# Moving stores to other queues and reordering the loads of an attention layer's input stage

## The chip, the cores and the metric

The program runs on one core of a Trainium2 chip. The core has a matrix engine (PE), a vector engine (DVE), a scalar engine (ACT), a general engine (POOL) and an engine that mostly issues DMAs (SP). Each engine takes its instructions strictly in the order in which they were written down for it; an instruction that waits holds everything behind it on that engine. A DMA is issued from the queue of SP, ACT or POOL; the issuing instruction stands in that engine's order like any other, and waits there for its source. The metric is the device time of one execution, in microseconds (us), lower being better.

## The reference, cut to what matters

Two layers on a latent stream `x` (1024 tokens x 1024 channels) and a context stream `ctx` (256 tokens). Layer 0 is multi-head latent attention, layer 1 a Hyena long convolution. What is computed around the change:

```python
shift, scale, gate = split(silu(c) @ ada_w[i] + ada_b[i], 3)      # adaLN, for each layer i
a  = modulate(rmsnorm(x,   norm_g[0]), shift,   scale)            # h * (1 + scale) + shift
ac = modulate(rmsnorm(ctx, norm_g[0]), shift_c, scale_c)
cq, ckv, k_rope, gate = split(a @ w_in, ...)                      # layer 0's input projections
h  = sin-MLP(features) @ w_out * exp(-t * deltas)                 # Hyena's filters, from the weights alone
spec = rfft(k_circ)                                               # their spectra, used only in layer 1
```

The filter spectra don't depend on `x`; the kernel computes them in layer 0's input stage, beside the projections.

## The kernel before, in words

`layer0_in` is the input stage; after it come attention, its output projection, and the Hyena layer. Everything is float32, products are made from a high and a low part with three matmuls each (`mm3`, lines L119 to L121). Activations lie with channels on partitions, in tiles of 128x512, the two halves of the tokens apart.

Three streams of work are interleaved in `layer0_in`:

- **The normalised input.** `load_x` loads a half of `x` (8 tiles), `rms` squares it on ACT (L380), sums over partitions on PE and forms the reciprocal root; `spread` puts that into a PSUM bank R (L414), and `modulate` makes the high and low part of the modulated input from it (DVE L421, ACT L422, DVE L423; 8 times for each half and, in narrower tiles, for the context).
- **adaLN.** `ada` loads blocks of `ada_w` (L156) and multiplies them with silu(c) in four packed column groups (L128). Layer 0's shift and scale (32 loads of 256 KB into `pg` tiles) come first, since `modulate` needs their result `gs`; layer 1's shift and scale and both gates come later, through two buffers `aw` of 512 KB each.
- **The filters.** `filters` loops over 8 groups g of channels. For each it makes 8 blocks j (matmuls `ph` L318/L319; a load `dec` through two buffers, L314; DVE `kk` L321, `kp`, `km`), and then the ring: DVE builds eight blocks `blk` (L222, L225), each is split by ACT into `bh` (L96) and by DVE into `bl` (L97), multiplied by the tables `fm` (`u`), brought from PSUM by ACT into one of two buffers `ko` (L340), and stored to DRAM as `kd` by two DMAs (L351; for one of the eight also two of `kx`, L353). The tables `fm` are loaded once, from POOL's queue (L295).

The projections take their weights through `weights()`: a load `wr` (L112), an ACT cast and a DVE subtraction. `gates` stores its result to `gate_d` (L600), `hilo_out` stores the compressed keys to `ckv_d` and `kr_d` (L514, L515). Except for `fm`, all loads and stores of this stage are issued from SP's queue. A scheduler sets the order of the instructions on each engine when the program is built, starting from the order in which the generators are advanced: one step of `filt` at a time, and one step of `todo` for every two of those. `keep_in_program_order` and `issue_after` pin an instruction; in the kernel before, `late` pinning is used only in the final norm.

Of the kernel before, what the change touches and what calls it, by code (L numbers as in the profile page):

```python
# [11 lines left out]
F32 = mybir.dt.float32  # L12
F32R = mybir.dt.float32r
AF = mybir.ActivationFunctionType
ALU = mybir.AluOpType
# [4 lines left out]
P = 128  # L20
D = 1024
L = 1024
LC = 256
NK = L + LC
KD = D // P
# [30 lines left out]
class Net:  # L56
# [85 lines left out]
        self.adac = [(self.cst.tile([P, 24, 2], F32, name=f"adac{i}"), self.cst.tile([P, KD, 2], F32, name=f"gs{i}"))  # L142
                     for i in range(2)]

    def ada(self, parts, page, bank, width):

        nc = self.nc
        ps = bank()
        for k in range(KD):
            cols = []  # L150
            for layer, first, n in parts:
                for s in range(0, n * 512, width):
                    wd = min(width, n * 512 - s)
                    w = page(wd)
                    o = 512 * first + s
                    nc.sync.dma_start(out=w, in_=self.a["adaw"][layer, k, :, o : o + wd])  # L156
                    cols += [w[:, j : j + 512] for j in range(0, wd, 512)]
            self.packed([(ps[32 * q : 32 * q + 32, :], self.sc[:, k, :], w, k == 0, k == KD - 1)
                         for q, w in enumerate(cols)])
            yield  # L160
        row = page(512)
        nc.scalar.copy(out=row, in_=ps)
        tp = bank().rearrange("p (j c) -> p j c", j=4)
        for j in range(4):
            nc.tensor.transpose(out=tp[:, j], in_=row[:, j * P : (j + 1) * P], identity=self.ident)
        q = 0
        for layer, first, n in parts:
            res, gs = self.adac[layer]
            for r in range(2):
                c = slice(4 * first, 4 * first + 4 * n)  # L170
                nc.vector.tensor_tensor(out=res[:, c, r].rearrange("p (q j) -> p j q", j=4),
                                        in0=tp[:, :, 32 * q + r : 32 * (q + n) : 32],
                                        in1=self.col(f"b{layer}", 4 * first, 4 * n).rearrange("p (q j) -> p j q", j=4),
                                        op=ALU.add)
                if first == 0:
                    nc.vector.scalar_tensor_tensor(out=gs[:, :, r], in0=res[:, 8:16, r], scalar=1.0,
                                                   in1=self.col(f"g{layer}", 0, 8), op0=ALU.add, op1=ALU.mult)
            q += n
# [105 lines left out]
    def filters(self, psum, pt_h, pt_u, side):  # L284
# [7 lines left out]
        for c in (slice(13, 19), slice(19, 25), slice(0, 7), slice(7, 13)):  # L292
            for i in range(2):
                nc.gpsimd.tensor_copy(out=fm[i][0:1, c.start, 0:1], in_=last[0:1, 0:1])
                nc.gpsimd.dma_start(out=fm[i][:, c], in_=a["fm"][i][:, c])  # L295
# [12 lines left out]
        for g in range(KD):  # L308
            wh, wl = nxt
            kp = [gp.tile([P, 4, CS], F32, tag="rg", name=f"kp{i}") for i in range(2)]  # L310
            km = [gp.tile([P, 4, CS], F32, tag="rg", name=f"km{i}") for i in range(2)]
            for j in range(8):
                dec = rp.tile([P, 2, 1, P], F32, tag="dec", name="dec", bufs=2)
                nc.sync.dma_start(out=dec, in_=a["dec"][g, j])  # L314
                ps = psum.tile([P, 2, 2, P], F32, tag=pt_h, name="ph")
# [21 lines left out]
            def emit(i, b):  # L337
# [10 lines left out]
                    nc.vector.memset(ko[0:1, 1], 0.0)  # L348
                for o in range(2):
                    oc = slice(P * o, P * o + P)  # L350
                    nc.sync.dma_start(out=self.kd[o, g // 2, :, r0 : r0 + 2, cl], in_=ko[:, :, oc])  # L351
                    if i == 0:
                        nc.sync.dma_start(out=self.kd[o, g // 2, :, 2, cl], in_=kx[:, oc])  # L353
# [64 lines left out]
    def modulate(self, x, R, gs, sh, hi, lo):  # L418
# [3 lines left out]
        nc.scalar.activation(out=hi, in_=x, func=AF.Identity, bias=sh)  # L422
        nc.vector.scalar_tensor_tensor(out=lo, in0=x, scalar=sh, in1=hi, op0=ALU.add, op1=ALU.subtract)  # L423

    def project(self, srcs, bank):

        nk = len(srcs[0][0])
# [27 lines left out]
    def layer0_in(self):  # L455
# [28 lines left out]
            for k in range(4):  # L484
                nc.sync.dma_start(out=xc[k], in_=a["ctxT"][:, 2 * k : 2 * k + 2, :])

        load_x(0)
        rx = [self.rms(x[0], 512, bank, page)]
        filt.send(x[0][7])
        for n, _ in enumerate(self.ada([(0, 0, 4)], lambda n: page(), abank, 512)):  # L490
            next(filt)
            if n == 7:
                load_x(1)
                rx.append(self.rms(x[1], 512, bank, page))
        load_c()
        xcs = [xc[k // 2][:, LC * (k % 2) : LC * (k % 2) + LC] for k in range(KD)]
        rc = self.rms(xcs, LC, bank, page)
        ax = []
        for xs, r in zip(x, rx):
            R = self.spread(r, 4, bank)  # L500
            hl = [[], []]
            for k in range(KD):
                hi, lo = page(F32R), page(F32R)
                self.modulate(xs[k], R, gs[:, k, 0:1], res[:, k, 0:1], hi, lo)
                hl[0].append(hi)
                hl[1].append(lo)
            ax.append(hl)

        def hilo_out(t, n, dsts):

            w = t.shape[-1]
            hi, lo = page(F32R)[:, :w], t.bitcast(F32R)
            self.split(t[:n], hi[:n], lo[:n])
            nc.sync.dma_start(out=dsts[0], in_=hi.bitcast(F32)[:n])  # L514
            nc.sync.dma_start(out=dsts[1], in_=lo.bitcast(F32)[:n])  # L515

        def normed(xs, g, dst, sl, sbuf=False):
            n = sl.stop - sl.start
# [10 lines left out]

        def context():  # L530

            R = self.spread(rc, 2, bank)
            ac = [[], []]
            for k in range(0, KD, 2):
                hi, lo = page(F32R), page(F32R)
                for q in range(2):
                    sl = slice(LC * q, LC * q + LC)
                    self.modulate(xcs[k + q], R[:, :LC], gs[:, k + q, 1:2], res[:, k + q, 1:2], hi[:, sl], lo[:, sl])
                    ac[0].append(hi[:, sl])
                    ac[1].append(lo[:, sl])  # L540
            yield
# [52 lines left out]
        def gates(ms):  # L594
            for m in ms:
                bs = yield from self.project(ax, bank)
                for b, sl in zip(bs, halves):
                    t = st()
                    act.activation(out=t, in_=b, func=AF.Silu)
                    nc.sync.dma_start(out=self.gate_d[m, :, sl], in_=t)  # L600
                yield

        def work():
            gen = chain(self.ada([(1, 0, 4)], awt, abank, 1024), self.ada([(0, 4, 2), (1, 4, 2)], awt, abank, 1024))
            for _ in gates(range(0, 3)):
                next(gen, None)
                yield
            yield from latent_kv()
            for _ in gates(range(3, 5)):
                next(gen, None)  # L610
                yield
            yield from context()
            for _ in gates(range(5, 6)):
                next(gen, None)
                yield
            for _ in gen:
                pass

        todo = work()
        n = 0  # L620
        for step, _ in enumerate(filt):
            while n * 120 < (step + 1) * 60:
                next(todo, None)
                n += 1
        for _ in todo:
            pass
        raws = []
        for c in (slice(1152, 2176), slice(0, 768), slice(768, 1152)):
# [819 lines left out]
```

## Time and profile before

| | us |
|---|---|
| median of three runs (lowest, highest) | 1737.97 (1730.38, 1744.37) |
| the profiled execution | 1731.71 |
| its span on the core | 1729.9 |
| PE busy, of the span | 1633.5 |
| DVE busy | 1442.2 |
| ACT busy | 766.3 |
| POOL busy | 16.0 |

The span is the time from the first to the last instruction on the core; 1.8 us of the execution lie outside it. Busy times of an engine are unions of its instructions. The input stage reaches from 0 to 430.4 us, where the first matmul of the attention stage (`pj` from `ckv` and `wc`) starts. The rows "SPq" are issues of DMAs on SP's queue; a row with "xN" merges N instructions in a row.

### The profile page before, as it was taken

To read this page: it belongs to the slowest core of one execution; us is meant where nothing else is said; L and a number is where in the kernel's file an instruction comes from. 1 tells how busy PE (TensorE), PEld (TensorE's weight loads), DVE (VectorE), ACT (ScalarE), POOL (GpSimd) and SP (SyncE) were. 2 spreads that over 40 slices of the span, in tenths; PEclk is the share of its full clock that TensorE was granted. 3 is DMA by queue.
4 is the path that set the end of the run, shared out by engine and by line. 5 is a ranking of instruction groups with operands and counts; after the bars stand their busy time and mean duration, and the time that the engine had idled before them with its cause. 6 is when DMAs were issued, how large, how long until landed. Compare 5 with 4: busy or idle time off the path is not lost.

```text
span 1729.9 us, 22940 instructions
## 1 busy us (share of the span) xinstructions
PE 1633.5 (94%) x8160; PEld 1299.5 (75%) x8160; DVE 1442.2 (83%) x2558; ACT 766.3 (44%) x1337; POOL 16.0 (1%) x43
## 2 busy tenths in 40 slices
PE   5899897899999999999999999999999999999996
PEld 2467676787788788788787777888888888887874
DVE  4886979895699899899899456999999999999856
ACT  4533444445455465555555345433433433343313
POOL 1000000000000000000000010000000000000000
PEclk9899999899999999999999999999999999999998
DMA  9777664436101001010014771332332332244545
GB/s 342 256 231 222 200 187 120 138 89 206 28 27 37 25 32 38 19 33 25 25 56 132 232 254 64 101 98 83 101 115 83 104 106 89 95 122 134 180 142 197
DMA packets 140759, 206.15 MB, mean 119 GB/s; under 512 B 13578, under 2 KB 71649, under 8 KB 140516
## 3 DMA queue, kind: packets, MB, share of 16 engines
q1 hardware_dynamic: 137508, 194.00, 35.7%
q0 software_dynamic: 3136, 10.69, 1.9%
q8 instruction: 64, 1.05, 0.3%
q14 instruction: 51, 0.42, 0.1%
HBM read 148.92 MB, written 53.61 MB: 117 GB/s over the span
## 4 chain that ended last, share of the span: by engine, by line
PE 75%; DVE 10%; DMA 9%; ACT 3%; issue 2%; SPq 1%; DVEq 0%; ACTq 0%
PE pj L121 12%; PE pj L119 12%; PE pj L120 12%; DMA dec<-in_dec 2%; PE O L120 2%; PE S L119 2%; PE O L119 2%; PE S L826 2%; PE O L121 2%; PE apx L762 2%; PE S L825 2%; PE S L121 2%; PE S L120 2%; PE apx L763 2%; PE fu L119 2%; PE fy L119 2%
## 5 line engine op out<-in xcount | busy, mean ns | idle before, releaser
L96 ACT CAST w<-wr 128x512 fp32r<-128x512 f32 (+1 forms) x149 | 90.7, 609 | 259.5 <-PE pj L120 129.5
L119 PE MATMUL pj<-a,w 128*128 128x512 f32 x512 | 203.1, 397 | 1.7 <-ACT a L422 1.6
L121 PE MATMUL pj<-a,w 128*128 128x512 f32 x512 | 203.1, 398 | 0.0
L120 PE MATMUL pj<-a,w 128*128 128x512 f32 x512 | 203.0, 397 | 0.0
L828 ACT ACTIVATE p<-S 128x512 f32<-128x512 f32 x160 | 95.7, 598 | 148.2 <-DVE acc L835 69.5
L97 DVE TENSOR_TENSOR w<-wr,w 128x512 fp32r<-128x512 f32 (+1 forms) x149 | 98.8, 671 | 54.7 <-ACT w L96 54.6
L96 ACT CAST bh<-raw 128x512 fp32r<-128x512 f32 x128 | 77.1, 620 | 89.1 <-DVE raw L1071 71.0
L119 PEld LDWEIGHTS pj<-a,w 128*128 128x128 f32 x512 | 96.4, 188 | 22.0 <-ACT a L422 2.4
L120 PEld LDWEIGHTS pj<-a,w 128*128 128x128 f32 x512 | 96.5, 188 | 19.9 <-DVE a L423 0.2
L121 PEld LDWEIGHTS pj<-a,w 128*128 128x128 f32 x512 | 96.6, 189 | 19.5 <-issue 0.8
L97 DVE TENSOR_TENSOR p<-p 128x512 fp32r<-128x512 f32 x160 | 109.4, 684 | 1.5 <-ACT p L96 1.2
L764 DVE TENSOR_REDUCE cm<-apx 128x1 f32<-128x512 f32 (+1 forms) x192 | 107.1, 591 | 3.8 <-PE apx L763 3.1
L835 DVE TENSOR_TENSOR acc<-acc,p 128x512 f32<-128x512 f32 x144 | 98.7, 685 | 7.6 <-ACT p L828 6.7
L121 PE MATMUL pj<-pg,w 128*128 128x512 f32 (+1 forms) x248 | 96.5, 389 | 8.7 <-DVE w L97 8.6
L96 ACT CAST p<-p 128x512 fp32r<-128x512 f32 x160 | 99.5, 622 | 4.8
L119 PE MATMUL pj<-pg,w 128*128 128x512 f32 (+1 forms) x248 | 95.7, 389 | 2.7 <-ACT pg L422 2.7
L120 PE MATMUL pj<-pg,w 128*128 128x512 f32 (+1 forms) x248 | 96.6, 389 | 0.6 <-DVE pg L423 0.6
L97 DVE TENSOR_TENSOR bl<-raw,bh 128x512 fp32r<-128x512 f32 x128 | 84.7, 686 | 9.1 <-ACT bh L96 9.0
L119 PE MATMUL u<-bh,fm 128*128 128x256 f32 (+1 forms) x200 | 68.2, 342 | 12.2 <-ACT bh L96 9.5
L762 PE MATMUL apx<-kn,qn 128*128 128x512 f32 (+1 forms) x192 | 69.0, 364 | 2.2 <-DVE cm L764 1.9
L321 DVE TENSOR_TENSOR kk<-ph,dec 128x512 f32<-128x512 f32 x64 | 42.6, 684 | 33.2 <-DMA dec<-in_dec 26.6
L763 PE MATMUL apx<-krh,r 128*128 128x512 f32 (+1 forms) x192 | 67.1, 357 | 0.0
(312 smaller groups left out, 4408.9 us busy)
## 6 DMA issues: line engine op xcount, KB each, us to landing
aw<-in_adaw SPq DMA_DIRECT2D x32, 512.0 KB
kd<-ko SPq DMA_DIRECT2D x128, 128.0 KB
wr<-in_hw SPq DMA_DIRECT2D x64, 256.0 KB
kt<-kd SPq DMA_DIRECT2D x56, 256.0 KB
wr<-in_w SPq DMA_DIRECT2D x34, 256.0 KB
dec<-in_dec SPq DMA_DIRECT2D x64, 128.0 KB
pg<-in_adaw SPq DMA_DIRECT2D x32, 256.0 KB
wr<-in_wo SPq DMA_DIRECT2D x32, 256.0 KB
```

The costliest lines, as they stand in the source:

```text
L96: self.nc.scalar.copy(out=hi, in_=raw)
L97: self.nc.vector.tensor_tensor(out=lo, in0=raw, in1=hi, op=ALU.subtract)
L119: mm(out, lhsT=w[0], rhs=x[0], start=start, stop=False)
L120: mm(out, lhsT=w[0], rhs=x[1], start=False, stop=False)
L121: self.last = mm(out, lhsT=w[1], rhs=x[0], start=False, stop=stop)
L321: nc.vector.tensor_tensor(out=kk, in0=ps, in1=dec.broadcast_to([P, 2, 2, P]), op=ALU.mult)
L762: mm(b[:, :w], lhsT=qn[0][:, c], rhs=kn[0][:, o : o + w], start=True, stop=False)
L763: mm(b[:, :w], lhsT=r1[:, c], rhs=krh[:, o : o + w], start=False, stop=True)
L764: v.tensor_reduce(out=cm[:, t, i : i + 1], in_=b[:, :w], axis=AX.X, op=ALU.max)
L825: mm(S, lhsT=krh[:, c], rhs=r1, start=False, stop=False)
L828: act.activation(out=p, in_=S, func=AF.Exp, scale=ASCALE)
L835: v.tensor_tensor(out=acc, in0=acc, in1=p, op=ALU.add)
```

## The change

Six edits, all in the input stage:

1. The stores `kd` and `gate_d` are issued from ACT's queue, `ckv_d` and `kr_d` from POOL's.
2. Layer 0's adaLN loads: four of the eight k (16 of 32 loads) are written ahead of the load of x's second half, the others behind it. Only three instead of eight filter steps are taken beside them.
3. The tables `fm` are loaded inside the first group, at j = 4. They wait for `last`, a tile of x, which DVE has by then overwritten.
4. x is multiplied by its reciprocal root as soon as that is known (`normalize`, one DVE product per tile), and `shifted` replaces `modulate`: ACT forms the high part from x * gs + shift directly, DVE forms the same in place (a tensor_scalar) and subtracts. The context's `rms` moves into `context()`.
5. The later adaLN work no longer advances inside `work()` but every second step from the eighth on; its loads keep their program order, and its packed matmuls are pinned behind the last projection or filter matmul.
6. The generator `ada` yields between the loads and the matmuls.

```diff
-    def ada(self, parts, page, bank, width):
+    def ada(self, parts, page, bank, width, late=True):
...
-                    nc.sync.dma_start(out=w, in_=self.a["adaw"][layer, k, :, o : o + wd])
+                    dma = nc.sync.dma_start(out=w, in_=self.a["adaw"][layer, k, :, o : o + wd])
+                    if late:
+                        self.tc.keep_in_program_order(dma)
                     cols += [w[:, j : j + 512] for j in range(0, wd, 512)]
-            self.packed([(ps[32 * q : 32 * q + 32, :], self.sc[:, k, :], w, k == 0, k == KD - 1)
-                         for q, w in enumerate(cols)])
             yield
+            with self.behind() if late else ExitStack():
+                self.packed([(ps[32 * q : 32 * q + 32, :], self.sc[:, k, :], w, k == 0, k == KD - 1)
+                             for q, w in enumerate(cols)])
...
             for j in range(8):
+                if (g, j) == (0, 4):
+                    for c in (slice(13, 19), slice(19, 25), slice(0, 7), slice(7, 13)):
+                        for i in range(2):
+                            nc.gpsimd.tensor_copy(out=fm[i][0:1, c.start, 0:1], in_=last[0:1, 0:1])
+                            nc.gpsimd.dma_start(out=fm[i][:, c], in_=a["fm"][i][:, c])
...
-                    nc.sync.dma_start(out=self.kd[o, g // 2, :, r0 : r0 + 2, cl], in_=ko[:, :, oc])
+                    nc.scalar.dma_start(out=self.kd[o, g // 2, :, r0 : r0 + 2, cl], in_=ko[:, :, oc])
...
+    def normalize(self, xs, r, bank):
+
+        n = xs[0].shape[-1]
+        R = self.spread(r, n // P, bank)
+        for x in xs:
+            self.nc.vector.tensor_tensor(out=x, in0=x, in1=R[:, :n], op=ALU.mult)
+
+    def shifted(self, x, gs, sh, hi, lo):
+
+        nc = self.nc
+        nc.scalar.activation(out=hi, in_=x, func=AF.Identity, scale=gs, bias=sh)
+        nc.vector.tensor_scalar(out=x, in0=x, scalar1=gs, scalar2=sh, op0=ALU.mult, op1=ALU.add)
+        nc.vector.tensor_tensor(out=lo, in0=x, in1=hi, op=ALU.subtract)
...
-        load_x(0)
-        rx = [self.rms(x[0], 512, bank, page)]
+        for h, xs in enumerate(x):
+            load_x(h)
+            self.normalize(xs, self.rms(xs, 512, bank, page), bank)
+            if h == 0:
+                first = self.ada([(0, 0, 4)], lambda n: page(), abank, 512, False)
+                for _ in range(4):
+                    next(first)
         filt.send(x[0][7])
-        for n, _ in enumerate(self.ada([(0, 0, 4)], lambda n: page(), abank, 512)):
-            next(filt)
-            if n == 7:
-                load_x(1)
-                rx.append(self.rms(x[1], 512, bank, page))
+        for n, _ in enumerate(first):
+            if n < 3:
+                next(filt)
...
-            nc.sync.dma_start(out=dsts[0], in_=hi.bitcast(F32)[:n])
+            nc.gpsimd.dma_start(out=dsts[0], in_=hi.bitcast(F32)[:n])
...
-                    nc.sync.dma_start(out=self.gate_d[m, :, sl], in_=t)
+                    nc.scalar.dma_start(out=self.gate_d[m, :, sl], in_=t)
...
         todo = work()
+        vecs = chain(self.ada([(1, 0, 4)], awt, abank, 1024), self.ada([(0, 4, 2), (1, 4, 2)], awt, abank, 1024))
...
                 next(todo, None)
                 n += 1
+                if n > 8 and n % 2:
+                    next(vecs, None)
```

Where the orders change. First SP's queue in the middle of the stage, in each program at the load `fwr` of the fifth group's filter weights (`dec` is the load of a decay block, `kd` the store of a filter block, `aw` a later adaLN load, `wr` a weight load). Before:

```order
L303 DMA fwr<-in_fwout 128x512 [waits DVE_49]
L112 DMA wr<-in_w 128x512 [waits DMAHW3_49,DVE_49]
L314 DMA dec<-in_dec 128x256 [waits DMAHW0_49,DVE_49]
L314 DMA dec<-in_dec 128x256 [waits DMAHW5_49,DMAHW1_49,DVE_49]
L351 DMA kd<-ko 128x2x128 [waits Activation_49]
L351 DMA kd<-ko 128x2x128 [waits DMAHW7_49]
L324 DMA hbias<-in_hbias 1x2x128 [waits DVE_49]
L351 DMA kd<-ko 128x2x128 [waits Activation_49]
L351 DMA kd<-ko 128x2x128 [waits DMAHW2_49]
```

Now, with no store among them:

```order
L318 DMA dec<-in_dec 128x256 [waits DMAHW0_49,DVE_49]
L302 DMA fwr<-in_fwout 128x512 [waits DVE_49]
L156 DMA aw<-in_adaw 128x1024 [waits DMAHW7_49,DMAHW6_49,PE_49]
L156 DMA aw<-in_adaw 128x1024 [waits PE_49]
L318 DMA dec<-in_dec 128x256 [waits DMAHW2_49,DMAHW1_49,DVE_49]
L328 DMA hbias<-in_hbias 1x2x128 [waits DMAHW3_49,DVE_49]
L156 DMA aw<-in_adaw 128x1024 [waits DMAHW7_49,DMAHW2_49,PE_49]
L156 DMA aw<-in_adaw 128x1024 [waits DMAHW6_49,DMAHW3_49,PE_49]
L318 DMA dec<-in_dec 128x256 [waits DMAHW5_49,DMAHW4_49,DVE_49]
```

The stores are gone from between the loads; the pinned `aw` loads, which wait for PE, stay among them. Second, ACT in a ring. Before, eviction and cast alternate:

```order
L96 CAST bh<-blk 128x512 [waits DVE_49] x2
L340 ACTIVATE ko<-u 128x512 [waits DMAHW1_49,PE_49]
L96 CAST bh<-blk 128x512 [waits DVE_49,Activation_49]
L422 ACTIVATE pg<-pg,adac_87 128x256 [waits DVE_49]
L340 ACTIVATE ko<-u 128x512 [waits DMAHW5_49,PE_49]
L96 CAST bh<-blk 128x512 [waits Activation_49]
```

Now:

```order
L344 ACTIVATE ko<-u 128x512 [waits PE_49]
L96 CAST bh<-blk 128x512 [waits DVE_49]
L355 DMA kd<-ko 128x2x128 [waits DMAHW0_49,Activation_49]
L355 DMA kd<-ko 128x2x128 [waits DMAHW2_49]
L344 ACTIVATE ko<-u 128x512 [waits DMAHW1_49,PE_49]
L96 CAST bh<-blk 128x512 [waits DVE_49]
L355 DMA kd<-ko 128x2x128 [waits DMAHW3_49,Activation_49]
L355 DMA kd<-ko 128x2x128 [waits DMAHW4_49]
L344 ACTIVATE ko<-u 128x512 [waits DMAHW2_49,DMAHW0_49,PE_49]
```

Two issues stand between an eviction and the one after the next cast; a name DMAHW in a row's brackets is a wait for an earlier DMA to have landed. Third, SP's queue at the start. Before, layer 0's adaLN loads come in one run with `dec` loads between them, and x's second half behind:

```order
L156 DMA pg<-in_adaw 128x512 x8
L314 DMA dec<-in_dec 128x256
L156 DMA pg<-in_adaw 128x512 x4
L314 DMA dec<-in_dec 128x256
L156 DMA pg<-in_adaw 128x512 x4
L314 DMA dec<-in_dec 128x256
```

Now (behind 16 adaLN loads and the 8 loads of x's second half):

```order
L318 DMA dec<-in_dec 128x256 [waits DMAHW3_49,DVE_49]
L318 DMA dec<-in_dec 128x256 [waits DMAHW4_49,DVE_49]
L302 DMA fwr<-in_fwout 128x512 [waits DMAHW5_49,Activation_49]
L112 DMA wr<-in_w 128x512 [waits DMAHW6_49,DVE_49]
L112 DMA wr<-in_w 128x512 [waits DMAHW7_49,DVE_49]
L318 DMA dec<-in_dec 128x256 [waits DMAHW3_49,DMAHW0_49,DVE_49]
L318 DMA dec<-in_dec 128x256 [waits DMAHW4_49,DMAHW1_49,DVE_49]
```

The second 16 adaLN loads stand behind these, and behind one more `wr` load that waits for DVE. From the attention stage on (6229 of PE's 7984 instructions, 1867 of DVE's, 1000 of ACT's) the order is the same in both programs on PE, DVE and ACT.

More of the change, by code (lines that the diff above doesn't have):

```diff
@@ L291, in filters @@
         last = yield
[L292 to L295, printed above, removed]
         two = lambda tag, dt=F32: rp.tile([P, 2, CS], dt, tag=tag, name=tag)
@@ L350, in emit @@
                     oc = slice(P * o, P * o + P)
-                    nc.sync.dma_start(out=self.kd[o, g // 2, :, r0 : r0 + 2, cl], in_=ko[:, :, oc])
+                    nc.scalar.dma_start(out=self.kd[o, g // 2, :, r0 : r0 + 2, cl], in_=ko[:, :, oc])
                     if i == 0:
-                        nc.sync.dma_start(out=self.kd[o, g // 2, :, 2, cl], in_=kx[:, oc])
+                        nc.scalar.dma_start(out=self.kd[o, g // 2, :, 2, cl], in_=kx[:, oc])
             for i, b in self.ring(two, lambda: gp.tile([P, 1024], F32, tag="rg", name="rg"), kp, km, False):
@@ L485, in load_c @@
                 nc.sync.dma_start(out=xc[k], in_=a["ctxT"][:, 2 * k : 2 * k + 2, :])
-        load_x(0)
-        rx = [self.rms(x[0], 512, bank, page)]
-        filt.send(x[0][7])
-        for n, _ in enumerate(self.ada([(0, 0, 4)], lambda n: page(), abank, 512)):
-            next(filt)
-            if n == 7:
-                load_x(1)
-                rx.append(self.rms(x[1], 512, bank, page))
+        for h, xs in enumerate(x):
[5 more added lines that the diff above has]
+                    next(first)
+        filt.send(x[0][7])
+        for n, _ in enumerate(first):
+            if n < 3:
+                next(filt)
         load_c()
         xcs = [xc[k // 2][:, LC * (k % 2) : LC * (k % 2) + LC] for k in range(KD)]
[L497 to L501, printed above, removed]
+        ax = [[[], []] for _ in halves]
+        for hl, xs in zip(ax, x):
             for k in range(KD):
                 hi, lo = page(F32R), page(F32R)
-                self.modulate(xs[k], R, gs[:, k, 0:1], res[:, k, 0:1], hi, lo)
+                self.shifted(xs[k], gs[:, k, 0:1], res[:, k, 0:1], hi, lo)
                 hl[0].append(hi)
                 hl[1].append(lo)
-            ax.append(hl)
         def hilo_out(t, n, dsts):
@@ L513, in hilo_out @@
             self.split(t[:n], hi[:n], lo[:n])
-            nc.sync.dma_start(out=dsts[0], in_=hi.bitcast(F32)[:n])
-            nc.sync.dma_start(out=dsts[1], in_=lo.bitcast(F32)[:n])
+            nc.gpsimd.dma_start(out=dsts[0], in_=hi.bitcast(F32)[:n])
+            nc.gpsimd.dma_start(out=dsts[1], in_=lo.bitcast(F32)[:n])
         def normed(xs, g, dst, sl, sbuf=False):
@@ L530, in context @@
         def context():
-            R = self.spread(rc, 2, bank)
+            self.normalize(xcs, self.rms(xcs, LC, bank, page), bank)
+            yield
             ac = [[], []]
@@ L537, in context @@
                     sl = slice(LC * q, LC * q + LC)
-                    self.modulate(xcs[k + q], R[:, :LC], gs[:, k + q, 1:2], res[:, k + q, 1:2], hi[:, sl], lo[:, sl])
+                    self.shifted(xcs[k + q], gs[:, k + q, 1:2], res[:, k + q, 1:2], hi[:, sl], lo[:, sl])
                     ac[0].append(hi[:, sl])
@@ L599, in gates @@
                     act.activation(out=t, in_=b, func=AF.Silu)
-                    nc.sync.dma_start(out=self.gate_d[m, :, sl], in_=t)
+                    nc.scalar.dma_start(out=self.gate_d[m, :, sl], in_=t)
                 yield
         def work():
[L604 to L607, printed above, removed]
+            yield from gates(range(0, 3))
             yield from latent_kv()
-            for _ in gates(range(3, 5)):
-                next(gen, None)
-                yield
+            yield from gates(range(3, 5))
             yield from context()
[L613 to L617, printed above, removed]
+            yield from gates(range(5, 6))
         todo = work()
+        vecs = chain(self.ada([(1, 0, 4)], awt, abank, 1024), self.ada([(0, 4, 2), (1, 4, 2)], awt, abank, 1024))
         n = 0
@@ L624, in layer0_in @@
                 n += 1
-        for _ in todo:
+                if n > 8 and n % 2:
+                    next(vecs, None)
+        for _ in chain(todo, vecs):
             pass
```

## The prediction

> **What bounds the kernel now.** I first read the busy times by stage (window, PE busy with its instructions, weight loads, DVE, ACT, POOL, granted clock, DMA share, GB/s):
>
> ```profile
> 0.00:30.00 30.00, 17.35 (x52) 6.64 (x53) 14.32 (x34) 18.82 (x30) 5.91 (x20) 0.91 0.96 322
> 30.00:60.00 30.00, 17.84 (x95) 6.56 (x94) 19.92 (x40) 4.72 (x8) 0.00 (x0) 0.78 1.02 368
> 60.00:110.00 50.00, 44.56 (x249) 28.97 (x249) 41.23 (x89) 29.31 (x55) 0.00 (x0) 0.95 0.64 196
> 110.00:400.00 290.00, 262.38 (x1433) 210.97 (x1430) 241.11 (x508) 124.35 (x225) 0.00 (x0) 0.96 0.55 166
> 400.00:430.40 30.40, 26.87 (x124) 21.19 (x123) 13.12 (x26) 12.30 (x21) 3.70 (x7) 0.94 0.79 236
> 430.40:1729.90 1299.50, 1264.54 (x6217) 1025.17 (x6215) 1112.54 (x1866) 576.83 (x1000) 6.42 (x16) 0.99 0.29 92
> ```
>
> Behind 430.4 us PE is busy 97% of the time, and the change leaves that part's order on PE, DVE and ACT as it is. So the answer is how far the point 430.4 moves. In the first 60 us the DMAs bound (share 0.96 and 1.02, 368 GB/s), and PE and DVE wait for them. From 110 to 400 no engine is full: PE lacks 290.0 - 262.4 = 27.6 us, DVE 290.0 - 241.1 = 48.9 us, ACT is busy 43%. That is a stage of waits. The view of waits names them (who waited for what: us in total, times, longest), first SP's queue from 60 us on, then DVE from 30 us on, then ACT and PE:
>
> ```profile
> SPq L351 <- ACT ko L340: 53.1, 32, 13.0
> SPq L112 <- DVE w L97: 30.4, 12, 15.7
> SPq L314 <- DVE kk L321: 23.8, 20, 10.7
> SPq L156 <- DMA aw<-in_adaw: 16.5, 6, 6.0
> DVE w L97 <- ACT w L96: 12.8, 4, 7.7
> DVE bl L97 <- ACT bh L96: 11.3, 14, 2.7
> ACT w L96 <- DMA wr<-in_w: 25.4, 11, 8.9
> ACT ko L340 <- DMA kd<-ko: 20.6, 13, 5.7
> PE u L119 <- ACT bh L96: 9.5, 5, 7.5
> ```
>
> For 53.1 us the head of SP's queue is a `kd` store that waits for ACT, with `dec`, `wr` and `aw` loads behind it. From 60 us on, the tile view of `dec` says what that costs DVE:
>
> ```profile
>   DMA dec<-in_dec: 16.7, 10
> ```
>
> A stretch of SP's queue shows it: after two `dec` issues that took 11.43 us with their waits, loads come only between stores (start, us with the waits between, what):
>
> ```profile
> 168.60 11.43 SPq L314 DMA_DIRECT2D dec<-in_dec  x2
> 181.22 1.02 SPq L351 DMA_DIRECT2D kd<-ko  x2
> 182.29 0.58 SPq L324 DMA_DIRECT2D hbias<-in_hbias  x1
> 182.91 3.55 SPq L351 DMA_DIRECT2D kd<-ko  x4
> 187.03 0.35 SPq L156 DMA_DIRECT2D aw<-in_adaw  x1
> 187.47 0.89 SPq L351 DMA_DIRECT2D kd<-ko  x2
> 188.46 0.48 SPq L314 DMA_DIRECT2D dec<-in_dec  x1
> ```
>
> **Part by part: the front (edits 2 to 4).** The marks are the result `gs` and the last product of the modulation:
>
> ```profile
> 68.18 0.14 DVE L176 SCALAR_TENSOR_TENSOR gs<-adac,cols 128x8 f32<-128x8 f32 x1
> 75.64 0.74 DVE L421 SCALAR_TENSOR_TENSOR pg<-pg,gs,pj 128x512 f32<-128x512 f32 x1
> 100.47 0.73 DVE L423 SCALAR_TENSOR_TENSOR pg<-pg,adac 128x512 fp32r<-128x512 f32 x1
> 8.34 0.43 DVE L205 TENSOR_SCALAR nrnd<-arg 128x512 f32<-128x512 f32 x1 [4.79 <-ACT arg L203]
> 8.80 0.69 DVE L206 TENSOR_TENSOR arg<-arg,nrnd 128x512 f32<-128x512 f32 x1
> 28.62 0.14 DVE L407 TENSOR_TENSOR rms<-rms 128x4 f32<-128x4 f32 x1
> ```
>
> Before, the modulation ends at 100.47 + 0.73 = 101.2 us. Now x's first half has its reciprocal root at 28.8 again. DVE then forms 8 products (8 x 0.69 = 5.5), two `w` (1.4), and `kk`, `kp`, `km`; the `wr` load ahead of the second 16 adaLN loads waits for DVE's third `w`, which I put at about 41 us. The second 16 adaLN loads (16 x 0.26 = 4.2 MB) take 11.4 us at 368 GB/s. The tables `fm` (3.3 MB, 8.9 us at that rate) are no longer issued at 13.9 but behind the first products, about 36 us, so they collide with those loads in part: I let 4 us of them count. That puts the loads' end near 57 us and `gs` at about 59, 9 us earlier. From there to the end of the modulation DVE's new order has 16 tensor_scalar, 16 subtractions and the first ring's work. The rows above give 0.43 and 0.69 by duration; successive products start 0.06 to 0.07 apart less than that, so 16 x (0.37 + 0.62) = 15.8, and about 17 us for the ring's 30 operations; with 2 us for waits it ends at 94. The gain is 101.2 - 94 = **7 us**. The 8 + 8 products of `normalize` cost 11.0 us of DVE, but DVE is idle for 10 us of the window from 30 to 60 and for 15.7 of that before, so they are hidden; without that cover they would cost those 11 us. Against `modulate` (two operations of 0.74) the modulation itself gets shorter by 16 x (0.74 + 0.73 - 0.43 - 0.69) = 5.6 us, which is in the 94. Bounds: no gain if the second loads land as late as `gs` stood (68.2), and -20 if they land as early as the data allow, at about 46 us.
>
> **SP's queue without stores (edit 1).** The stores taken off:
>
> ```profile
> L351 SPq DMA_DIRECT2D kd<-ko x128: 355/460/1446, 63.8 to 407.4; - x128
> L353 SPq DMA_DIRECT2D kd<-kx x16: 326/438/543, 102.8 to 401.8; - x16
> ```
>
> 128 + 16 `kd` and 16 `gate_d` make 160 issues of 0.46 us, 74 us of SP; the 18 stores of `hilo_out` go to POOL, where nothing is queued behind them until the `ckv` loads at 403.8. SP's own issue time isn't what bounds; the waits at its head are. DVE's waits for `dec` (16.7) and, through ACT, for `wr` (12.8 at `w`) can fall at most to zero: 29.5 us. At least nothing is won, where the instruction behind waits for something else. What is late next is PE, which lacks only 27.6 us in this stage. I take **-20**: all of the 16.7 and a quarter of the 12.8, nearer the upper bound since the rows say that DVE stands there, and PE has work in hand.
>
> The page DMA: Bandwidth & Descriptors of the Trainium skill, section Issuing engines are not separate DMA queues, speaks against this: all three queues end on the same 16 DMA engines, and issuing from several saves only the issue time. By that rule this term would be 0, and the change would be worth its front alone. The rule doesn't count the head of a queue that waits for an engine, and that wait is what the 53.1 us row shows.
>
> **The stores on ACT.** Every ring step on ACT was a cast and an eviction; now it has two issues more, and the order puts a wait for an earlier DMA's landing at most of them. Behind an issue that waits stand the next eviction and cast, for which PE's `u` and DVE's `bl` wait. The rows (ACT, one ring):
>
> ```profile
> 355.40 0.60 ACT L340 ACTIVATE ko<-u 128x512 f32<-128x512 f32 x1 [2.02 <-PE u L121]
> 355.89 0.61 ACT L96 CAST bh<-blk 128x512 fp32r<-128x512 f32 x1
> 356.58 0.60 ACT L340 ACTIVATE ko<-u 128x512 f32<-128x512 f32 x1
> 369.10 1.11 ACT L340 ACTIVATE ko<-u 128x512 f32<-128x512 f32 x2 [3.17 <-PE ph L319]
> ```
>
> From the first to the eighth eviction (369.6) are 14.2 us, so a step takes 2.0 us. ACT's share of it is 0.50 + 0.50 (the starts of successive instructions), and two issues at SP's 0.46 bring it to 1.9. So ACT alone just fits, if no issue waits. An issue on ACT isn't in this trace; SP's is the nearest row. With w us of waiting per step the 64 steps grow by 64 x (w - 0.1). I take w = 0.2: **+6**. Bounds: -10 (half of ACT's 20.6 us of waits for `kd` landings, since the stores now leave at once) and +50 (w = 0.9).
>
> **The pinned adaLN work (edits 5 and 6).** 64 loads and 64 matmuls stay. Their loads follow each release by PE, and PE takes the packed matmul in its fixed place; in the new order 27 to 98 PE instructions lie between release and use. At the mean spacing of the window from 110 to 400 (290.0/1433 = 0.202 us) that is 5.5 us at the shortest, a little less than one landing took in the chain of waits:
>
> ```profile
> 93.94 6.36 DMA aw<-in_adaw
> ```
>
> So some of the 16 will wait a little: **+2**, between 0 and 16.
>
> **The end of the stage.** The last `kd` lands late, DVE's `cq` waits for it, then PE (chain of waits, then PE):
>
> ```profile
> 407.45 11.45 DMA kd<-ko
> 423.69 0.68 PE L121 MATMUL pj<-pg,w 128*128 128x512 f32 x1 [3.53 <-DVE w L97]
> ```
>
> The order keeps the `ckv` loads beside the last stores, so I leave this as it is: 0, between -5 (PE's 3.5 us and the slower matmuls behind them) and +5.
>
> **The sum:** -7 - 20 + 6 + 2 + 0 = -19 us. The profiled execution took 1731.7 (span 1729.9 and 1.8 outside), so 1712.7. The median of the three runs lies 6.3 above that execution, so I expect a median of 1737.97 - 19 = **1719.0**.
>
> **Rivals.**
>
> *ACT becomes the queue that stops everything: slower.* The mechanism is w. Where stores wait on ACT as they did on SP (53.1 us over 64 steps is 0.83 us per step), the term is 64 x (0.83 - 0.1) = 47 in place of 6, and the sum is -7 - 20 + 47 + 2 = +22: 1760. It decides from w = 0.5 on: 64 x 0.4 = 26, what the other terms win. For it: casts and evictions feed both busy engines, and a landing took up to 11.45 us above. Against it: ACT is the engine that most of those SP waits were for, and once it issues itself it waits only for landings.
>
> *No change: the waits only move.* `dec` and `wr` come early, but PE and DVE, at 90% and 83% in the middle, wait for each other in the same fixed interleaving, and the `aw` loads, which wait for PE, still stand on SP's queue ahead of `dec`. Then only half of the front and little else shows: -7 + 6 + 2 - 5 = -4, 1734. For it: 16.5 us at `aw` in the SP rows. Against it: 53.1 us at `kd`, three times as much, are gone. The page of the Trainium skill named above would land here too: with its 0 for the queue the sum is -7 + 0 + 6 + 2 = +1, 1739.
>
> *All of it.* w = 0, ACT's 20.6 us halve, the front reaches -15, and the middle falls to PE's work (-27): -15 - 27 - 10 + 2 = -50, less what overlaps; about -42, 1696.
>
> **How the numbers follow.** About 1%, 17 us, is what a measurement of this kernel can tell from no change; the three runs alone spread over 14. Forecast (-11 to -30): 0.50, some seven tenths of it beyond -17. All of it: 0.10. No change (-10 to +6): 0.23. ACT as the queue (+6 to +40): 0.17. Faster is 0.35 + 0.10, and 0.02 of the no-change case, where the front alone reaches its bound of -20: 0.47. Slower is 0.14, since a sixth of that rival stays under +17. The same has the rest: 0.15 + 0.21 + 0.03 = 0.39. The range leaves out the deep half of the best case and the upper two thirds of the slow one: 1694 to 1750.
>
> **What would show it.** Right: `gs` near 59 us and the modulation's end near 94; `dec` waits of DVE under 5 us behind 60; no wait of SP for `ko`; ring steps of 2.0 to 2.2 us on ACT; the first `ckv` matmul at about 411. Wrong: ACT idle ahead of its `kd` issues for more than 0.5 us a step, with PE's waits for `bh` above 9.5; or SP standing at `aw` for much more than 16.5; or `gs` later than 68.

## The result, and the profile after

| | us |
|---|---|
| before, median of 4 runs (lowest, highest) | 1736.19 (1730.38, 1744.37) |
| changed, median of 4 runs (lowest, highest) | 1754.16 (1752.66, 1756.94) |
| ratio changed to before, 95% interval | 1.0096, 1.0076 to 1.0116 |
| span of the profiled execution, before and changed | 1729.9, 1750.9 |
| first `ckv` matmul, before and changed | 430.4, 452.1 |

The change made the kernel 0.96% slower, where 1719 was forecast. In the two profiled executions the whole loss lies in the input stage: it ends 21.7 us later, and what follows takes 1298.8 us instead of 1299.5. (The profiled execution before lies 4.5 us under its median and the changed one 1.5, so these 21.7 us stand against 18.0 between the medians.)

Where in the stage it went is seen by counting. The first two rows are windows of the kernel before, the last two of the changed kernel (window, then length, then PE busy with its matmul count, PE weight loads, DVE, ACT, POOL, granted clock, DMA share, GB/s); the second window of each ends where the stage ends:

```profile
0.00:110.00 110.00, 79.75 (x393) 42.17 (x393) 75.46 (x160) 52.85 (x92) 5.91 (x20) 0.89 0.83 277
110.00:430.40 320.40, 289.25 (x1555) 232.17 (x1552) 254.23 (x533) 136.66 (x245) 3.70 (x7) 0.96 0.58 173
```

```profile
0.00:110.00 110.00, 77.01 (x303) 43.35 (x304) 74.26 (x157) 47.94 (x76) 9.95 (x20) 0.78 0.64 213
110.00:452.10 342.10, 302.99 (x1643) 235.83 (x1643) 262.28 (x560) 143.65 (x264) 13.49 (x25) 0.95 0.60 183
```

By 110 us PE has done 303 matmuls instead of 393. The count overstates the loss, since 48 of the 90 are products of the later adaLN work. They take 6.4 us of PE before, and in the changed kernel the fifth edit puts them behind 110 us (the first at 129.6). The group in the kernel before, up to 110 us (busy us, mean ns, idle us before it):

```profile
L128 PE MATMUL ad<-aw,sc 128*32 128x512 f32 x48 | 6.4, 604 | 4.4 <-DMA aw<-in_adaw 4.4
```

A fairer measure is full-clock time: PE's busy time less the share of it that the trace's clock records show as withheld, which is half where the granted clock is 0.50 and nothing elsewhere. (Successive 512-wide products of the changed kernel start 0.43 us apart at 73.8 us, at half clock, and 0.23 apart at 82.2, at the full one.) By this measure the stage is the same work in both kernels, 349.6 and 350.0 us. Three points tell where the time went:

- By 110 us the kernel before has done 69.7 us of this work, the changed one 58.3. So 11.4 us are lost there: 8.7 of clock and 2.7 of idle time.
- When the sixth of the eight filter rings starts on PE, both have done 236.9 us of it (236.8 changed), at 308.6 and at 328.5. So from 110 us to there 8.4 us more are lost, 5.9 of them idle time.
- Behind that point 1.9 us are lost.

Over the whole stage PE is idle for 72.1 us instead of 61.4 and busy for 380.0 instead of 369.0, so about half of the loss is clock and half idle time. The middle of the stage, on which the forecast put its largest gain, became slower.

What happens up to 110 us stands in the changed kernel's order in time, first POOL, then PE:

```profile
80.01 5.30 POOL L315 CAST fm<-pg 1x1 fp32r<-1x1 f32 x8 [79.57 <-DVE pg L440]
85.26 4.50 POOL L316 DMA_DIRECT2D fm<-in_fm  x8
```

```profile
66.43 0.50 PE L120 MATMUL pj<-pg,w 128*128 128x512 f32 x1 [2.44 <-DVE pg L441]
...
73.22 0.80 PE L120 MATMUL pj<-pg,w 128*128 128x512 f32 x1 [0.61 <-DVE pg L441]
73.81 0.63 PE L121 MATMUL pj<-pg,w 128*128 128x512 f32 x1
74.24 0.63 PE L119 MATMUL pj<-pg,w 128*128 128x512 f32 x1
...
82.19 0.40 PE L121 MATMUL pj<-pg,w 128*128 128x512 f32 x1
82.42 0.39 PE L119 MATMUL pj<-pg,w 128*128 128x512 f32 x1
...
89.21 0.77 PE L119 MATMUL u<-bh,fm 128*128 128x512 f32 x1 [5.47 <-DMA fm<-in_fm]
```

The tables `fm` are issued at 85 us; the first ring product `u` runs at 89.2, before at 59.8. From 63 us until then PE has only the projection's products, three for each tile that DVE modulates, and nothing for the last 5.5 us. The windows of that time show the rest:

```profile
70.00:80.00 10.00, 7.73 (x15) 4.03 (x15) 10.00 (x21) 1.81 (x3) 0.00 (x0) 0.50 0.00 0
80.00:90.00 10.00, 4.45 (x16) 2.83 (x15) 7.92 (x18) 4.14 (x6) 9.74 (x16) 0.84 0.46 142
```

From 70 to 80 us DVE is full, PE runs at half clock, and the DMAs move nothing at all.

The waits of DVE from 60 us to the stage's end, before and then changed (who waited for what: us, times, longest):

```profile
DVE kk L321 <- DMA dec<-in_dec: 16.7, 10, 5.2
DVE w L97 <- ACT w L96: 12.8, 4, 7.7
DVE bl L97 <- ACT bh L96: 11.3, 14, 2.7
...
DVE kk L321 <- PE ph L319: 6.1, 4, 2.1
```

```profile
DVE bl L97 <- ACT bh L96: 24.5, 13, 7.1
DVE kk L325 <- PE ph L323: 19.4, 8, 5.7
...
DVE w L97 <- ACT w L96: 9.5, 9, 3.1
DVE kk L325 <- DMA dec<-in_dec: 9.0, 11, 1.8
```

The two waits that the stores on SP's queue were to have caused fall from 29.5 to 18.5 us, and the other two rise from 17.4 to 43.9. Nor did the head of SP's queue come free. No store waits there any more, but the pinned `aw` loads do. From 60 us to the stage's end, beside the 16.5 us of the prediction's rows, the kernel before has

```profile
SPq L156 <- PE ad L128: 10.4, 11, 1.2
```

and the changed kernel, with PE's waits for `bh` (9.5 before) below:

```profile
SPq L156 <- PE ad L128: 31.7, 14, 6.2
SPq L156 <- DMA aw<-in_adaw: 19.1, 6, 5.1
SPq L156 <- PE pj L418: 14.3, 1, 14.3
PE u L119 <- ACT bh L96: 23.7, 12, 8.3
```

These are 65.1 us at `aw` instead of 26.9, where `kd` had stood for 53.1. What they cost can't be read from the rows, since DVE's waits for `dec` fell all the same.

### The profile page after: what moved, and what is told of

Same layout as the page of the kernel before. It is cut to its first block, busy times and chain, and to the rows that moved or that the text cites. A ratio compares the mean times of both kernels' runs of the same rounds, so it can differ in the third digit from the quotient of the medians.

```text
span 1750.9 us, 22892 instructions
## 1 busy us (share of the span) xinstructions
PE 1643.2 (94%) x8160; PEld 1303.4 (74%) x8160; DVE 1449.1 (83%) x2582; ACT 768.4 (44%) x1339; POOL 29.4 (2%) x61
## 4 chain that ended last, share of the span: by engine, by line
PE 76%; DVE 9%; DMA 7%; ACT 3%; issue 1%; ACTq 0%; POOL 0%; SPq 0%; DVEq 0%
PE pj L119 13%; PE pj L121 13%; PE pj L120 12%; PE apx L774 2%; PE apx L775 2%; PE O L120 2%; PE S L119 2%; PE O L119 2%; PE O L121 2%; PE S L838 2%; PE S L837 2%; PE S L121 2%; PE S L120 2%; PE fu L119 2%; PE fy L119 2%; PE fy L121 2%
## 5 line engine op out<-in xcount | busy, mean ns | idle before, releaser
L840 ACT ACTIVATE p<-S 128x512 f32<-128x512 f32 x160 | 95.7, 598 | 147.6 <-DVE acc L847 68.7
L119 PE MATMUL u<-bh,fm 128*128 128x256 f32 (+1 forms) x200 | 68.1, 340 | 29.2 <-ACT bh L96 23.7
L344 ACT ACTIVATE ko<-u 128x512 f32<-128x512 f32 x64 | 38.2, 598 | 71.8 <-PE u L121 44.5
```

What stands on the lines that cost most here:

```text
L119: mm(out, lhsT=w[0], rhs=x[0], start=start, stop=False)
L344: nc.scalar.activation(out=ko, in_=u, func=AF.Copy, scale=1.0 / 1024)
L840: act.activation(out=p, in_=S, func=AF.Exp, scale=ASCALE)
```

## The experiments

"Before" is always run beside the kernels on the same chip; the ratios are to it. A shorthand for the three switches on top of the front edits (2, 3, 4 and 6): the tables **late** (at j = 4, as changed) or **early** (at j = 3); the **stores** moved (edit 1) or on SP; the later adaLN work **pinned** (edit 5) or free.

| kernel | median | ratio, 95% interval |
|---|---|---|
| changed: late, moved, pinned | 1754.2 | 1.0096, 1.0076 to 1.0116 |
| e1: early, moved, pinned | 1749.9 | 1.0075, 1.0051 to 1.0099 |
| e2: late, on SP, pinned | 1749.0 | 1.0072, 1.0048 to 1.0095 |
| f4: late, moved, free | 1748.7 | 1.0072, 1.0046 to 1.0099 |
| e3: early, on SP, pinned | 1752.7 | 1.0083, 1.0056 to 1.0110 |
| f3: early, moved, free | 1750.1 | 1.0086, 1.0060 to 1.0113 |
| m1: late, on SP, free | 1746.5 | 1.0057, 1.0039 to 1.0075 |
| f2: early, on SP, free | 1737.8 | 1.0000, 0.9982 to 1.0019 |
| e4: before, all stores moved | 1747.4 | 1.0064, 1.0047 to 1.0082 |
| h2: before, only `kd` on ACT | 1738.7 | 1.0002, 0.9984 to 1.0020 |
| h1: before, only gates on ACT, keys on POOL | 1735.8 | 0.9996, 0.9982 to 1.0010 |
| p1: before, `kd` and gates on ACT | 1741.5 | 1.0017, 0.9999 to 1.0036 |
| f1: before, edits 5 and 6 alone | 1730.0 | 0.9957, 0.9926 to 0.9989 |
| k2: f1 and `kd` on ACT | 1734.4 | 0.9993, 0.9976 to 1.0011 |

### Undoing one part of the change

The tables one step earlier (e1):

```diff
-                if (g, j) == (0, 4):
+                if (g, j) == (0, 3):
```

> The changed kernel with the tables fm loaded one filter step earlier (at j = 3 of the first group, written ahead of the in-place modulation of x instead of behind it). Theory T, the tables came late: POOL's copy waits only for the first product on x, near 38 us instead of 80.0; the first ring matmul starts near 78 us, when its blocks are split, instead of 89.2; DMAs no longer idle from 70 to 85; the stage ends 12 to 18 us earlier, time 1736 to 1743. Rival Q, the stores on ACT's queue cost the time: nothing but the first ring moves, 1750 to 1756. Rival P, the pinned adaLN work costs it: the same, 1750 to 1756.

1749.9: the theory's mechanism held, its size did not. The profile of e1, first ring products and the result `gs`:

```profile
L119 PE MATMUL u<-bh,fm x200: 274/283/796, 85.2 to 424.0; 128*128 128x256 f32 x72, 128*128 128x512 f32 x28
```

```profile
L179 DVE SCALAR_TENSOR_TENSOR gs<-adac,cols x4: 159/165/169, 68.7 to 220.3; 128x8 f32<-128x8 f32 x4
```

POOL's copy starts at 37.52 and the table loads are issued from 40.02. The tables now come early enough, but they share the DMAs with the second 16 adaLN loads, and PE waits 7.4 us for one of those; `gs` is at 68.7 where the changed kernel had it at 62.1 (before, 68.2). So `u` gains only 4 us, and by 110 us PE has 309 matmuls instead of 303. What one load gains another pays. The intervals of e1 and of the changed kernel overlap, so even 4 us are not certain; the same holds for e2 and f4 below.

The stores back on SP, alone (e2) and with the early tables (e3):

```diff
-                    nc.scalar.dma_start(out=self.kd[o, g // 2, :, r0 : r0 + 2, cl], in_=ko[:, :, oc])
+                    nc.sync.dma_start(out=self.kd[o, g // 2, :, r0 : r0 + 2, cl], in_=ko[:, :, oc])
```

and likewise for `kx`, `gate_d` (SP for ACT) and both `hilo_out` stores (SP for POOL).

> The changed kernel with all stores (kd, gate_d, ckv_d, kr_d) back on SP's queue, the late tables kept. Theory T: as slow as the changed kernel or slower; slower by the 14 us that the prediction gave the two queue terms (1768) if SP's queue with stores costs what was forecast, equal (1750 to 1758) if the queue is worth nothing. Rival Q: back to about the kernel before, 1732 to 1742.

> Both: tables one step earlier and all stores on SP's queue. With e1, e2 and the changed kernel a square of two by two. If the two act apart from each other, e3 is e1 + e2 - 1754. Theory T with the forecast for the queue: 1750 to 1757; T with a queue worth nothing: 1736 to 1743; rival Q: 1732 to 1742 whether the tables are late or not.

1749.0 and 1752.7. Neither the queue as forecast (which asked for 1768 in e2) nor the stores on ACT as the sole cause (1732 to 1742) stands. e3 has no late tables and no moved stores, and its interval overlaps the changed kernel's, so a third part has to matter. That led to the pins:

```diff
         def work():
-            yield from gates(range(0, 3))
+            gen = chain(self.ada([(1, 0, 4)], awt, abank, 1024), self.ada([(0, 4, 2), (1, 4, 2)], awt, abank, 1024))
+            for _ in gates(range(0, 3)):
+                next(gen, None)
+                yield
...
-                if n > 8 and n % 2:
-                    next(vecs, None)
```

with `late=False` throughout (f4); and, pinned as it is but from the first step on (k1), `if n % 2:` in place of `if n > 8 and n % 2:`.

> The changed kernel with the fifth edit undone (later adaLN loads and products free to be placed early, as in the kernel before); the stores stay on ACT and POOL, the tables stay late. Theory H, pinning takes away the only work that could fill the hole that the front edits leave from 60 to 110 us: the adaLN products (ad from aw) start near 70 us again, the DMAs move more than 190 GB/s in that window instead of 126, and the time falls by 10 to 18 us, to 1736 to 1744. Rival, the late tables and the stores hold it: 1750 or more.

> The changed kernel, pinned as it is, but the later adaLN work is taken every second step from the first step on instead of from the eighth. Theory H: it is the start that matters, so the time falls by half or more of what taking away the pins gives, to 1738 to 1748. Rival, the fixed places of the products cost PE by waiting for the loads: no gain, 1750 to 1758, with more PE time waiting for aw than 3.3 us.

1748.7 and 1750.9 (ratio 1.0089, 1.0065 to 1.0113). In f4 the adaLN products did start at 62.3 us and the DMAs moved 195 GB/s from 60 to 110, as that theory wanted, yet PE had only 174 matmuls in that window (changed 147, before 249), and the time barely moved. Filling the hole with loads and with those products is not what was missing. Theory H falls.

### Building the front up, one switch at a time

f2 is the front alone, tables early, stores on SP, adaLN work free. m1 turns the tables late, f3 moves the stores, and e3 above pins.

> The second to fourth edit alone (stores on SP, later adaLN work as in the kernel before, tables written one filter step earlier than in the changed kernel). Theory F: 1746 to 1753, as e3, with some 70 PE instructions fewer than the kernel before between 60 and 110 us. Theory P: 1732 to 1740. The prediction's term for the front was -7: 1729.

> The front edits as in the changed kernel (tables late), stores on SP, later adaLN work free. Against f2 (1737.8) this differs by the late tables alone. If the tables' 45 us matter by themselves: 1744 to 1752, with the first ring product near 88 us and 10 to 20 PE instructions fewer by 110 us than f2's 331. If other work fills PE while the tables are missing: 1735 to 1741.

> The front edits with early tables and later adaLN work free, and all stores moved as in the first edit. Against f2 (1737.8) this differs by the stores alone. If they cost as they did on the kernel before (e4, +11): 1746 to 1751. If they were worth what was predicted (-14): 1724. If nothing: 1735 to 1741.

1737.8, 1746.5 and 1750.1. This settles which parts of the change can carry the loss: from f2, each switch by itself costs (late tables +0.57%, moved stores +0.86%, pins +0.83%), and all three together cost 0.96%. They do not add, and undoing any one of them in the changed kernel gave little.

Where they cost shows against f2. Its window up to 110 us:

```profile
0.00:110.00 110.00, 75.56 (x331) 41.06 (x332) 73.06 (x154) 49.49 (x79) 7.09 (x20) 0.80 0.77 260
```

In full-clock time f2 has done 60.3 us of work by then, 9.4 less than the kernel before, and its stage ends at 438.9, 8.5 us late: behind 110 us it loses nothing more. m1, f3 and e3 are 7.7, 7.3 and 10.0 us behind at 110, much as f2 is, but their stages end 15.4, 19.9 and 21.5 us late. So in these profiles the switches cost behind 110 us, not ahead of it.

Why f2's median nevertheless equals that of the kernel before, its profile does not show. The profiled execution before lies 6 us under the median of the runs beside f2, f2's 1.8. And f2's part behind the stage was 4.1 us shorter than before (1295.4), where m1, f3 and e3 took 1298.0 to 1301.0 for it; the order on PE, DVE and ACT is the same there in all of them, so this looks like a difference between executions.

One place where PE stands idle behind 110 us is the start of a ring (changed kernel, PE, then DVE; a bracket is idle time and its releaser):

```profile
319.78 0.40 PE L323 MATMUL ph<-fw,hr 128*128 128x256 f32 x1
328.48 0.79 PE L119 MATMUL u<-bh,fm 128*128 128x512 f32 x1 [8.31 <-ACT bh L96]
329.24 0.80 PE L120 MATMUL u<-bl,fm 128*128 128x512 f32 x1
```

```profile
319.61 2.35 DVE L228 TENSOR_TENSOR rg<-kp,kp 128x1024 f32<-128x1024 f32 x2
321.87 1.29 DVE L228 TENSOR_TENSOR rt<-km,km 128x512 f32<-128x512 f32 x2
323.08 2.50 DVE L225 SCALAR_TENSOR_TENSOR rg<-rt,km 128x512 f32<-128x512 f32 x4
```

DVE builds a ring's blocks for 8 us, and unless projection products stand in PE's order at that moment, PE waits and comes back at half clock. The kernel before has one such hole (7.46 us, at 308.6), the changed one two above 5 us (5.49 at 281.0, 8.31 at 328.5). But f2 has two as well (7.67 and 8.43), so the holes at ring starts do not separate f2 from the others, and what does is not settled.

### More filter steps in the front

The front takes three filter steps beside the second adaLN loads, where the kernel before takes eight. g1 is e1 with eight, n1 is f2 with eight:

```diff
-            if n < 3:
+            for _ in range(2):
                 next(filt)
```

> The changed kernel with the tables one step earlier and with eight filter steps instead of three taken beside layer 0's second adaLN loads, as many as in the kernel before. Theory F: the first ring starts 8 to 15 us earlier than in e1 (85.2 there), and the time falls from 1750 to 1738 to 1743. Rival: the DMAs bound the front, so the steps taken earlier only push the adaLN loads back by what they load: 1747 to 1752.

> f2 with eight filter steps instead of three beside the second adaLN loads. If the ring's meeting with the modulation on DVE is the front's cost (theory F): the ring starts before 78 us and the time falls to 1728 to 1733, the -7 of the prediction. If the DMAs bound the front anyway: 1736 to 1741.

g1 gave 1743.9 (1.0036, 1.0018 to 1.0054) against 1749.9 for e1; `u` starts at 73.4 instead of 85.2. On f2, n1 gave 1742.9 (1.0034, 1.0016 to 1.0053), 5 us more than f2. By 110 us n1 has 348 matmuls against 331, and it still ends later: the steps helped on e1 and not on f2. A count at 110 us alone does not decide the time.

### Parts of the change on the kernel before

All stores moved (e4), only `kd` (h2), only gates and compressed keys (h1), `kd` and gates (p1): the same replacements of a queue as above, the other way round.

> The kernel before with only the first edit (kd and gate_d from ACT, ckv_d and kr_d from POOL). The prediction's two terms: -20 + 6 = -14, so 1722. The waits only move: 1732 to 1740. Rival Q (ACT becomes the queue): +10 or more, from 1746.

> The kernel before with only the kd stores moved to ACT's queue (gate_d, ckv_d and kr_d stay on SP's). Theory K, the two issues in every ring step cost the 11 us of e4: 1744 to 1750. Rival: they cost nothing and it was the 18 stores moved to POOL and the 16 of the gates: 1732 to 1739. The prediction's terms: -20 + 6, 1722.

> The kernel before with only gate_d on ACT and ckv_d and kr_d on POOL; kd stays on SP. If the parts of the first edit add up, it carries the 10 us that all stores cost and kd alone did not: 1744 to 1750. If they don't add up, but the two moves together only drive the order into a bad place: 1734 to 1740.

> The kernel before with kd and gate_d on ACT's queue, the compressed keys' stores on SP. If ACT's queue is what fills up by the two together: 1744 to 1750. If it was the pair with POOL's stores that made e4 slow: 1733 to 1740.

1747.4, 1738.7, 1735.8 and 1741.5. Moving `kd` is the part that removes the head of SP's queue, and it is worth nothing: the interval reaches from -0.16% to +0.20%. In h2 SP no longer waits for `ko`, and DVE's waits for `dec` fall from 16.7 to 10.1 us; its waits for `bh` rise from 11.3 to 14.4. What is left of the first edit is worth nothing either, and both together cost 0.64%, of which `kd` with the gates makes at most 0.36%. Here too the parts don't add. In e4 the waits moved the same way as in the changed kernel:

```profile
DVE bl L97 <- ACT bh L96: 20.1, 15, 4.1
DVE kk L321 <- PE ph L319: 15.8, 6, 7.6
...
DVE kk L321 <- DMA dec<-in_dec: 8.2, 10, 1.7
```

The pins alone (f1), and with `kd` on ACT (k2):

```diff
+                    if late:
+                        self.tc.keep_in_program_order(dma)
...
+            with self.behind() if late else ExitStack():
```

> The kernel before with the fifth and sixth edit alone (later adaLN work taken every second step from the eighth on, loads in program order, products pinned). Theory F, the front cost the time (the first ring and three quarters of the first group's filter steps were taken out of the DMA-bound first 60 us and now meet the modulation on DVE): 1732 to 1741, as the kernel before. Theory P, the pinned adaLN work costs it: 1746 to 1752. The prediction's term for it was +2.

> The kernel before with the fifth and sixth edit and the kd stores on ACT. If queue and pins help each other (with no stores ahead of them the pinned loads leave SP at once): 1722 to 1728. If kd on ACT is worth nothing: 1728 to 1732.

1730.0 and 1734.4. f1 is faster than the kernel before by 0.43% (0.11% to 0.74%). The same pins on f2's front cost 0.83% (e3). PE's waits for `aw` are 7.2 us before and 2.3 in f1. Adding `kd` to it seems to take the gain back, but the two intervals overlap (from 0.9976 to 0.9989), so this is not certain.

A caution for all these rows: moving even one kind of store gives the scheduler another problem, and it orders the stage anew. In the traces, with buffer numbers left out, `kd` alone moves 300 of the stage's 1,944 matmuls to another place in PE's order; on f2, turning the tables late moves 83 and moving the stores 213. So a part's cost here is that of its queue and of the order that comes with it. An experiment that moves the stores and holds the engines' order was not made, and whether the 10 us of e4 are queue or order stays open.

## Why the prediction was wrong

It forecast 1719 with a range from 1694 to 1750; 1754.2 is outside. By its own steps:

- **The tables at "about 36 us".** This is, in order of time, the first step that failed. The copy on POOL reads a tile of x, and I took the product of `normalize` for the write that it waits for. But the step j = 4 is written behind `shifted`, which writes the same tile again. The copy waited for that second write: 79.57 us of waiting, until 80.0. Its share of the loss can't be given as one number (4 us in the changed kernel, within the noise; 9 on f2). Nor is it simply PE's 5.5 us of waiting for the tables: at 110 us m1 is no further behind than f2.
- **The front, -7.** `gs` came at 62.1 (59 forecast), 6 us earlier. The modulation ended at 105.3 instead of 94, later than the 101.2 before. The sum counted DVE's operations (17 us of ring beside the modulation) and left out what PE has to do meanwhile: with the ring behind the modulation's start, PE has three products for each 2.3 us of DVE, at half clock. Its `tensor_scalar` took 0.54 us and not the 0.43 of the row that it was read from, 1.8 us over 16 of them. DVE also stood 7.07 us for `bh` until 95.0, since ACT waited for `u` and `u` for the tables. The front alone with early tables, f2, measured 1.0000; that is 0, at the end of the term's bounds (of the 9.4 us that its profile has lost by 110 us, 5.3 are clock). With the tables late, as the change has them, it is m1, +0.57%, and outside them.
- **SP's queue without stores, -20.** The mechanism did what it said: no wait for `ko` on SP, and the two waits named fell, by 11.0 of 29.5 us. The step that failed is "all of the 16.7 and a quarter of the 12.8" as a gain of time: the waits for `bh` and for `ph` took their place (+26.5). Measured, the term is 0 for `kd` (h2). This is the rival "the waits only move", which had 0.23, and the rule of the Trainium skill (DMA: Bandwidth & Descriptors, section Issuing engines are not separate DMA queues) that several issuing engines save only the issue time: h2 and h1 agree with the zero that it gives. All stores together (e4, +11) go beyond that rule to the slow side.
- **The stores on ACT, +6.** The ring rows on ACT are as forecast: evictions at 374.95, 376.59, 378.59, 381.26 and 382.90, a step of 2.0 us, and ACT's waits for `kd` landings at 20.0 (20.6 before). So w, on which the slower rival rested, stayed small in this ring. The rival's +22 has the sign and the rough size of the result (+18) by luck, not by its mechanism.

```profile
374.95 0.60 ACT L344 ACTIVATE ko<-u 128x512 f32<-128x512 f32 x1 [1.89 <-PE u L121]
375.45 0.61 ACT L96 CAST bh<-blk 128x512 fp32r<-128x512 f32 x1
375.58 0.89 ACTq L355 DMA_DIRECT2D kd<-ko  x2
376.59 0.60 ACT L344 ACTIVATE ko<-u 128x512 f32<-128x512 f32 x1 [0.54 <-PE u L121]
```

- **The pinned adaLN work, +2.** Wrong in sign on the kernel before (-0.43%), too small on the front (+0.83%). The forecast looked only at the waits for its loads, and those shrank (PE for `aw`: 7.2 us before, 3.3 changed).
- **The end of the stage, 0.** This held: from the start of the sixth ring to the stage's end, the same work, the kernel before needs 121.8 us and the changed one 123.6.
- **The signs that it named.** Of those for being wrong, SP's standing at `aw` came (65.1 us, 26.9 before). Of the one for ACT's queue only half came: PE's waits for `bh` rose to 23.7 us, but ACT idle ahead of its `kd` issues does not show in the ring above. `gs` was not late.
- **The sum.** Its terms were added as if each held on any base. The rows f2, m1, f3, e3 show that here they don't: three switches of 0.6 to 0.9% make 0.96% together.

Settled: in the profiles half of the loss lies before 110 us and nearly all of the rest ahead of the sixth ring, in clock as much as in idle time; the first edit is worth no gain; the front is worth none; any one of late tables, moved stores and pins brings the front from 1.000 to between 1.006 and 1.009. Not settled: by what mechanism each of them costs behind 110 us, why the second and third cost nothing more, and how much of each is the order that the scheduler makes of it.

## What to carry to other kernels

A load that is held back by reading a tile waits for the last write ahead of it in program order: look for every write of that tile, in-place ones too, before dating the load. Long waits of one queue were not time that could be won here, where PE and DVE were busy at 90% and 83%; count what the bounding engine has done by a point, weighed by its clock and not in instructions, and ask which work fills it. And where a scheduler re-orders everything, try each part of a change on the kernel before and on the changed one, since the two answers can differ in sign.

## What was not expected of the hardware

Half of the loss was PE's clock, and 5.1 us of clock were withheld from 67.2 to 80.85 us, a stretch without any long pause of PE; the kernel before has the full clock there. From 70 to 80 us PE was busy for 7.73 of 10 us, with gaps of 0.61 us every 2.3 us, and its granted clock stayed at 0.50 (a 512-wide product took 0.63 us; 0.40 at 82.19, when products had run back to back). The Trainium skill (TensorE: Matmul & The Clock Gate, Part 1) says that the full clock is given after some 3.4 us of sustained activity and withdrawn after an idle window of about that length; no gap in that stretch is as long, and the clock stayed low all the same, which agrees with the first half of the rule. The second half does not fit the start of the stretch: the clock was withdrawn at 67.20 after a gap of 2.44 us (63.99 to 66.43) and no longer one.

The trace suggests what decided here. The clock changed at 63.78, 67.20 and 80.85 us; one step is 3.42 us, the other four times 3.41. In the five stretches of that length PE was busy for 0.97, 1.93, 2.45, 2.72 and 3.06 us: after the first the full clock was withdrawn, after the next three it stayed away, after the last it came back. So some 80% busy was too little here and some 90% enough (PE's ends are modelled). A stream of products that another engine hands out one tile at a time was charged twice here: for its gaps, and for the half clock in between.
